# Summing the mean square per token, and moving the gate's modulation behind the fourth GLU pair

## The chip, the cores and the metric

The kernel runs on one core of a Trainium2 chip. The metric is device time in microseconds. The kernel before took 1121.05 us, the median of three runs (1117.35, 1121.05, 1123.47). The engines are named as the profile names them: PE is TensorE (PEld its weight loads), DVE is VectorE, ACT is ScalarE, POOL is GpSimd, SP is the engine that issues the DMAs here.

## What is computed

Two transformer blocks run one after the other on 512 tokens of width 1024. Only the entry of the first one matters here. `x` is normalised by its root mean square over the channels, scaled and shifted by a modulation that comes from the vector `c`, and projected; a third part of the modulation, `gate`, multiplies the block's output at its very end.

```
mod = silu(c) @ w_mod + b_mod
shift, scale, gate = split(mod, 3)
y = x * rsqrt(mean(x*x, axis=-1) + 1e-6)
u = (y * norm_w) * (1 + scale) + shift
p = u @ w_in          # q, k, v, attention gate, GLU halves, conv gate
a, g = split(p[GLU]); conv input = a * sigmoid(g)   # four pairs of 128 channels
...
h = x + gate * (concat(attention, conv) @ w_out)
```

## The kernel before

The kernel keeps channels on the partitions and tokens along the free axis: `x` is eight tiles `xs[j]` of 128 channels by 512 tokens. Each float32 product is made of three matmuls on rounded parts: a weight is split into `wh` (a rounded copy, made by ACT) and `wl` (the rest, made by DVE), the activations into the two tiles of `u`, and `mm3` multiplies high by high, high by low and low by high. Raw weights come in through two buffers (`wr`), the split ones stand in three (`wh`) and two (`wl`).

The instructions are written with a framework that orders them itself: a planner walks the program with its own estimate of every duration and, on each engine, takes the instruction that is ready and stands earliest in the program. So program order is a priority and not the order of execution, and each engine, the DMA issuer SP among them, then runs its list strictly in order. Only the depthwise convolution (`conv`) is marked to come later than its place in the program: its 120 multiply-adds on DVE fill what is free. Buffers of one tag are handed out in turn, and the next user of a buffer waits until the last reader of the one before is through. The PSUM tags of the first block are `pj` (one bank), `pv` (one), `pt` (two) and `s` (two pairs of banks).

The first block starts like this. Twelve matmuls on zeros (`warm_up`) open the PE. The eight tiles of `x` are loaded, then the modulation weights and the first raw weights. ACT squares each `xs[j]`, and PE multiplies the squares by a 128 x 128 matrix of 1/1024 (`ones`), adding the eight products in one `pj` bank: every partition then holds the mean square of all 512 tokens. ACT takes the root into `bs`, DVE the reciprocal of all 128 x 512 values.

The modulation is computed in six groups of 512 columns of `w_mod`. `mod_group` multiplies the vectors (32 columns, two used) with four loaded tiles, eight matmuls spread over the four 32-row strips of a `pj` bank; ACT copies the bank to `part`; four matmuls with two columns each turn the copy into per-partition scalars in a `pv` bank. `mod_pair` uses this for shift and scale of two channel tiles (groups 0 to 3), `mod_gate` for the gate (groups 4 and 5). Group 0 is done in two halves.

The loop `for j in range(KT)` then takes one channel tile after the other: it makes the modulation pair for every second j, `apply_mod` multiplies `xs[j]` by `bs` on DVE, scales and shifts it on ACT into `U` and takes the low part on DVE, and 18 matmuls add the products with six column blocks of the weights (`w_start`, three GLU pairs) into six banks `accs`: four on `s` and two on `pt`. After the loop, `glu` reads the three pairs (ACT a tanh, DVE a product), both gate groups are made, `conv` of the first three pairs is issued, and the fourth GLU pair is projected into `pj` and `pv` with the weights `w_in[0]` and `w_in[1]`, 24 matmuls each. The query projection (`q_ps`, on the banks `s`), the keys and values (on `pt`) and the attention with its gates (`zgate`, on `pj`, `pv` and `pt`) follow.

The helpers that the change newly calls exist before: `rsqrt` (ACT root, DVE reciprocal) and `bcast`, which spreads one column of per-token values over a row by a PE transpose for each 128 tokens. The context's norm (`norm_bs`) uses both with two columns.

Of the kernel before, what the change touches and what calls it, by code (L numbers as in the profile page):

```python
# [16 lines left out]
AF = mybir.ActivationFunctionType  # L17
# [5 lines left out]
P = 128  # L23
S = 512
D = 1024
KT = 8
# [198 lines left out]
def rsqrt(k, r, x, eps):  # L225
    k.A.activation(r, x, AF.Sqrt, bias=k.eps[eps])
    k.V.reciprocal(out=r, in_=r)
# [36 lines left out]
def bcast(k, r, n, tag):  # L264
    b = k.t(tag)
    for j in range(n):
        k.T.transpose(b[:, j * P:(j + 1) * P], r[:, j:j + 1].to_broadcast([P, P]), k.ident)
    return b
# [35 lines left out]
def setup1(k, I):  # L304
    k.rows = k.cal([6, 64])
    k.Y.dma_start(out=k.rows, in_=I["rows"].partition_broadcast(P))
    k.ones512 = k.cal([P])
    k.G.memset(k.ones512, 1.0 / 512)
    k.cw = small(k, k.vec("conv_w", 0, 124), 124, 0.5)
    k.hlw = small(k, k.vec("conv_ln_w", 0, 4), 4, 0.5)  # L310
    k.hlb = small(k, k.vec("conv_ln_b", 0, 4), 4, 0.5)
    k.bpw2 = small(k, k.vec("b_pw", 0, 4), 4, 2.0)
# [27 lines left out]
def block1(k, I, st, h1d):  # L340
    A, V, T, G, Y = k.A, k.V, k.T, k.G, k.Y
# [35 lines left out]
        Y.dma_start(out=t, in_=I["w_mod"][g, i])  # L377
        return t

    def mod_group(ts, e0=0, e1=2):  # L380
        ps = k.t("pj")
        o = slice(e0 * 256, e1 * 256)
        for kt in range(KT):
            q = 32 * (kt % 4)
            T.matmul(ps[q:q + 32, o], cc[:, kt, :], ts[kt // 2][:, kt % 2, o], start=kt < 4, stop=kt >= 4)
        part = k.t("tA")
        A.activation(part[:, o], ps[:, o], AF.Copy)
        cols = k.t("pv", [4, 2])
        for i in range(2 * e0, 2 * e1):
            T.matmul(cols[:, i, :], part[:, i * P:(i + 1) * P], k.sel32[:, 0:2], start=True, stop=True)  # L390
        return cols

    def mod_pair(g, ts, e0=0, e1=2):
        cols = mod_group(ts, e0, e1)
        for e in range(e0, e1):
            j = 2 * g + e
            V.tensor_scalar(out=shift[:, :, j], in0=cols[:, 2 * e, :], scalar1=k.vec("b_mod", j), scalar2=None, op0=ALU.add)
            V.tensor_scalar(out=A1[:, :, j], in0=cols[:, 2 * e + 1, :], scalar1=bm1[:, j:j + 1],
                            scalar2=k.vec("norm_w", j), op0=ALU.add, op1=ALU.mult)

    def mod_gate(g, ts):
        cols = mod_group(ts)
        V.tensor_tensor(out=gate[:, 4 * g - 16:4 * g - 12], in0=cols[:, :, 0], in1=k.vec("b_mod", 4 * g, 4), op=ALU.add)

    def norm_bs(vals, w, tag):
# [18 lines left out]
        V.tensor_tensor(out=lo, in0=t, in1=hi.bitcast(F32), op=ALU.subtract)  # L424
        return hi, lo

    ones = k.cal([P])
    G.memset(ones, 1.0 / D)
    ps = k.t("pj")
    for j in range(KT):  # L430
        sq = k.t("tA")
        A.activation(sq, xs[j], AF.Square)
        T.matmul(ps, ones, sq, start=j == 0, stop=j == KT - 1)
    bs = k.t("bs")
    A.activation(bs, ps, AF.Sqrt, bias=k.eps[1e-6])
    V.reciprocal(out=bs, in_=bs)
    a0, a1 = k.t("s", [2, S]), k.t("s", [2, S])
    accs = [a0[:, 0, :], a0[:, 1, :], a1[:, 0, :], a1[:, 1, :], k.t("pt"), k.t("pt")]
    us = []
# [1 line left out]
    mods = [[k.t("modw", [2, S]) for i in range(4)]]  # L441
# [36 lines left out]
    def glu(pa, pg):  # L478
        t = k.t("tA")
        A.activation(t, pg, AF.Tanh, scale=0.5)  # L480
        u2 = k.t("hg")
        V.scalar_tensor_tensor(out=u2, in0=t, scalar=1.0, in1=pa, op0=ALU.add, op1=ALU.mult)
        up.append(u2)
# [3 lines left out]
    def conv(i):  # L487
        u, cw = up[i], lambda w: k.cw[:, i * 31 + w:i * 31 + w + 1]
        y = ys[i] = k.t("hg")
        A.activation(y, u, AF.Identity, scale=cw(15), bias=k.vec("conv_b", i))  # L490
        with k.tc.high_priority(offset=-LATER):
            for w in range(31):
                if w != 15:
                    o0, o1 = max(0, 15 - w), min(S, S + 15 - w)
                    V.scalar_tensor_tensor(out=y[:, o0:o1], in0=u[:, o0 + w - 15:o1 + w - 15], scalar=cw(w), in1=y[:, o0:o1],
                                           op0=ALU.mult, op1=ALU.add)
# [4 lines left out]
    W1.fill(1)  # L501
    for i in range(3):
        glu(accs[2 * i], accs[2 * i + 1])
    for g in (4, 5):
        mod_gate(g, mods[g])
    setup1(k, I)
    k.rest()
    for i in range(3):
# [3 lines left out]
    proj(k, pg, W1.next(), us)  # L512
    glu(pa, pg)
    conv(3)

    q_ps = [k.t("s", [2, S]), k.t("s", [2, S])]
    for g in range(4):
        wh, wl = W1.next()
        for kk in range(2):
            j = 2 * g + kk  # L520
            c = slice(kk * S, (kk + 1) * S)
            for t in range(4):
                tt = slice(t * P, (t + 1) * P)
                uh, ul = us[j]
                ps = q_ps[t // 2][:, t % 2, :]
# [18 lines left out]
    for t in (2, 3, 4, 5, 0, 1):  # L544
        ps = k.t("pt", [256])
# [104 lines left out]
    for g in range(2):  # L650
        for o, ts_ in ((0, range(2, 6)), (512, range(0, 2))):
            b = k.t("pt")
# [120 lines left out]
    for pr in range(4):  # L773
        for half in range(2):
# [8 lines left out]
            if pend is not None:  # L783
                if pend[1] == 0:
                    pv = k.t("pv")
# [38 lines left out]
    for m in range(KT):  # L824
        if m % 2 == 0:
            wh, wl = W1.next()
        ps = oacc[m]
# [654 lines left out]
def emit(tc, I, out, dbg=None, stages=("b1", "b2", "ff")):  # L1482
    k = K(tc, dbg)
    nc = tc.nc
    with ExitStack() as st:
        k.open(st, "g", dict(g=1, wr=2, wh=3, wl=2))
        setup(k, I)
        h1d = nc.dram_tensor("h1d", (KT, P, S), F32, kind="Internal").ap()
        k.open(st, "H", dict(xa=6, xb=4, hg=16))
        p1 = ExitStack()  # L1490
        k.open(p1, "p1", dict(c1=1, U=16, tA=4, kvs=6))
        k.open(p1, "p1m", dict(pj=1), PSUM)
        k.open(p1, "p1s", dict(s=2), PSUM)
        k.open(p1, "p1t", dict(pt=2), PSUM)
        k.open(p1, "p1v", dict(pv=1), PSUM)
        if "b1" not in stages:
            k.rest()
        if "b1" in stages:
            nm = block1(k, I, p1, h1d)
        else:  # L1500
            nm = Norm(k, "norm_mix_g", "hg", "xb")
            for j in range(KT):
                x = k.x()
                k.Y.dma_start(out=x, in_=I["xT"][:, j, :])
                k.Y.dma_start(out=h1d[j], in_=x)
                nm.add(j, x)
        p1.close()
        k.nx = 0
        if "b2" in stages:
            k.open(st, "p2a", dict(c2=1, p=6, rk=4, v=2, z=2, bon=3, s8=6, nr=8))  # L1510
            k.open(st, "p2m", dict(pj=2), PSUM)
            k.consts("c2", 1350)
            block2(k, I, nm, h1d, out)
# [95 lines left out]
```

## Time and profile before

| | |
|---|---|
| runs | 1123.47, 1121.05, 1117.35 us; median 1121.05 us |
| the profiled execution | 1122.11 us, span 1120.3 us, mean granted PE clock 0.986 |
| PE busy | 1077.6 us, 96% of the span |
| PEld busy | 831.9 us, 74% |
| DVE busy | 727.6 us, 65% |
| ACT busy | 538.0 us, 48% |
| POOL busy | 61.8 us, 6% |

All times of the trace are microseconds from the start of the span. A granted clock of 1.00 is the PE's level of 2.4 GHz, 0.50 the level of 1.2 GHz. In a timeline row the bracket at the end says how long the engine had idled before and what ended it. A float32 matmul leaves two records. Every instruction of the kernel's helpers bears line 57, so instructions are told apart by their tiles: `s<-U,wh` is a matmul into `s` that reads `U` and `wh`. The span outside of the first 250 us (rest of the attention, output projection, second block and feed-forward) is not touched by the change.

### The profile page before, as it was taken

How to read it: one execution, taken by the hardware profiler on the slowest of the kernel's cores; microseconds unless marked ns; L12 is line 12 of the kernel's file. 1: busy time of each engine (PE TensorE's matmuls, PEld its weight loads, DVE VectorE, ACT ScalarE, POOL GpSimd, SP SyncE). 2: the span in 40 equal slices, each digit the busy share in tenths (PEclk: the TensorE clock that was granted, in tenths of full speed). 3: DMA queues.
4: the chain of work that ended last, by engine and by line, in shares of the span. 5: the costliest groups of instructions: out<-in, count | busy, mean ns of one | idle time of the engine just before them, and what ended most of it. 6: DMA issues, size and time to landing. Idle time of an engine off the chain costs nothing.

```text
span 1120.3 us, 15945 instructions
## 1 busy us (share of the span) xinstructions
PE 1077.6 (96%) x6272; PEld 831.9 (74%) x6272; DVE 727.6 (65%) x1267; ACT 538.0 (48%) x987; POOL 61.8 (6%) x209
## 2 busy tenths in 40 slices
PE   8999989999999999999999879999999999999998
PEld 4668966666787677777777657768888888888887
DVE  3369999995776889797867877666444344344332
ACT  5444546765655556555455655555333133134110
POOL 0000000000010201122101121010000000000000
PEclk9999999999999999999999998999999999999999
DMA  9753221001362110110011212122323333333332
GB/s 330 286 178 105 64 81 45 1 23 35 94 199 90 57 39 20 39 37 28 32 39 52 67 48 76 40 74 85 104 94 94 94 96 101 103 95 94 94 122 85
DMA packets 32203, 96.46 MB, mean 86 GB/s; under 512 B 3456, under 2 KB 6272, under 8 KB 32128
## 3 DMA queue, kind: packets, MB, share of 16 engines
q1 hardware_dynamic: 32128, 95.45, 26.5%
q8 instruction: 49, 0.80, 0.3%
q14 instruction: 26, 0.21, 0.1%
HBM read 91.24 MB, written 4.19 MB: 85 GB/s over the span
## 4 chain that ended last, share of the span: by engine, by line
PE 82%; DVE 6%; ACT 4%; POOL 3%; DMA 3%; issue 2%; SPq 0%; ACTq 0%; DVEq 0%; POOLq 0%
PE pf L57 31%; PE pj L57 22%; PE s L57 9%; PE i L57 7%; PE pt L57 5%; PE pv L57 4%; PE y L57 3%; POOL nr L57 3%; DMA modw<-w_mod 1%; ACT p L57 1%; DVE wl L57 1%; DVE hg L57 1%; ACT wh L57 1%; DVE p L57 1%; DMA wr<-w_in 1%
## 5 line engine op out<-in xcount | busy, mean ns | idle before, releaser
L57 ACT ACTIVATE wh<-wr 128x1024 fp32r<-128x1024 f32 (+1 forms) x132 | 137.7, 1043 | 183.7 <-PE pf L57 73.9
L57 DVE TENSOR_TENSOR wl<-wr,wh 128x1024 fp32r<-128x1024 f32 (+1 forms) x132 | 158.7, 1203 | 21.9 <-PE pt L57 10.2
L57 PE MATMUL pf<-A,wh 128*128 128x512 f32 x512 | 157.8, 389 | 0.0
L57 PE MATMUL pj<-hg,wh 128*128 128x512 f32 x448 | 152.5, 412 | 1.4 <-DVE x L57 0.9
L57 ACT ACTIVATE f<-i 128x512 f16<-128x512 f32 (+1 forms) x132 | 71.9, 598 | 90.1 <-PE i L57 89.9
L57 PEld LDWEIGHTS pf<-A,wh 128*128 128x128 f32 x512 | 96.0, 188 | 19.7
L57 PE MATMUL pf<-A,wl 128*128 128x512 f32 x256 | 99.6, 389 | 0.0
L57 DVE TENSOR_TENSOR x<-x,pf 128x512 f32<-128x512 f32 (+1 forms) x33 | 22.2, 671 | 113.9 <-PE pf L57 113.9
L57 PEld LDWEIGHTS pj<-hg,wh 128*128 128x128 f32 x448 | 80.2, 190 | 18.5 <-issue 2.2
L57 PE MATMUL pj<-hg,wl 128*128 128x512 f32 x224 | 90.2, 403 | 0.0
L57 DVE SCALAR_TENSOR_TENSOR hg<-hg,c 128x499 f32<-128x499 f32 (+14 forms) x120 | 84.9, 738 | 0.7 <-ACT hg L57 0.4
L57 PE MATMUL pf<-ff,wh 128*128 128x512 f32 (+1 forms) x272 | 79.6, 377 | 0.0
L57 PE MATMUL pf<-hg,wh 128*128 128x512 f32 x256 | 78.8, 389 | 0.0
L57 DVE SCALAR_TENSOR_TENSOR fr<-pf,r 128x512 f32<-128x512 f32 x32 | 22.1, 691 | 85.4 <-PE pf L57 82.1
L57 ACT ACTIVATE fr<-fr 128x512 f32<-128x512 f32 x32 | 20.2, 632 | 99.9 <-DVE fr L57 99.9
L57 PEld LDWEIGHTS <-f 128*128 128x128 f16 x720 | 46.8, 101 | 24.1 <-issue 13.7
L57 PE MATMUL i<-f 128*128 128x128 f16 x672 | 56.2, 226 | 5.3 <-DVE f L57 4.9
L57 PEld LDWEIGHTS pf<-ff,wh 128*128 128x128 f32 x272 | 50.1, 188 | 9.4
L57 PEld LDWEIGHTS pf<-A,wl 128*128 128x128 f32 x256 | 48.0, 188 | 10.1
L57 PEld LDWEIGHTS pf<-hg,wh 128*128 128x128 f32 x256 | 48.0, 188 | 9.9
L57 PE MATMUL pf<-ff,wl 128*128 128x512 f32 (+1 forms) x136 | 51.2, 376 | 0.0
L57 PE MATMUL pf<-hg,wl 128*128 128x512 f32 x128 | 49.8, 389 | 0.0
(312 smaller groups left out, 2114.8 us busy)
## 6 DMA issues: line engine op xcount, KB each, us to landing
wr<-w_ff SPq DMA_DIRECT2D x64, 512.0 KB, 3.5
modw<-w_mod SPq DMA_DIRECT2D x20, 512.0 KB, 7.6
wr<-rw_in SPq DMA_DIRECT2D x20, 512.0 KB, 3.6
wr<-w_in SPq DMA_DIRECT2D x10, 512.0 KB, 3.7
wr<-w_out SPq DMA_DIRECT2D x8, 512.0 KB, 3.6
wr<-w_start SPq DMA_DIRECT2D x8, 384.0 KB, 5.9
x<-xT SPq DMA_DIRECT2D x8, 256.0 KB, 5.8
modw<-w_mod SPq DMA_DIRECT2D x8, 256.0 KB, 6.2
```

The lines of the kernel that those rows point to most:

```text
L57: r = f(*a, **kw)
```

## The change

The squares become the stationary operand: for each of the eight squared tiles and each of the four 128-token blocks, one matmul with a single moving column of 1/1024 (`inv1k`) adds into one column of a `pt` bank (columns 0, 2, 4, 6), 32 matmuls in all. The tokens then lie on the partitions. `rsqrt` works on 128 x 4 values, `bcast` spreads the result with four transposes into the second `pt` bank, and ACT copies it to `bs`. The matrix `ones` and its memset are gone. The two gate groups move from behind the third GLU pair to behind the fourth one's `conv(3)`, ahead of the query projection, and take both of their banks from `pt` instead of `pj` and `pv`.

```diff
-    def mod_group(ts, e0=0, e1=2):
-        ps = k.t("pj")
+    def mod_group(ts, e0=0, e1=2, tags=("pj", "pv")):
+        ps = k.t(tags[0])
...
-        cols = k.t("pv", [4, 2])
+        cols = k.t(tags[1], [4, 2])
...
     def mod_gate(g, ts):
-        cols = mod_group(ts)
+        cols = mod_group(ts, tags=("pt", "pt"))
...
-    ones = k.cal([P])
-    G.memset(ones, 1.0 / D)
-    ps = k.t("pj")
+    ps = k.t("pt")
     for j in range(KT):
         sq = k.t("tA")
         A.activation(sq, xs[j], AF.Square)
-        T.matmul(ps, ones, sq, start=j == 0, stop=j == KT - 1)
+        for t in range(4):
+            T.matmul(ps[:, 2 * t:2 * t + 1], sq[:, t * P:(t + 1) * P], k.inv1k, start=j == 0 and t == 0, stop=j == KT - 1 and t == 3)
+    r = k.cal([4])
+    rsqrt(k, r, ps[:, 0:8:2], 1e-6)
+    b = bcast(k, r, 4, "pt")
     bs = k.t("bs")
-    A.activation(bs, ps, AF.Sqrt, bias=k.eps[1e-6])
-    V.reciprocal(out=bs, in_=bs)
+    A.activation(bs, b, AF.Copy)
...
     for i in range(3):
         glu(accs[2 * i], accs[2 * i + 1])
-    for g in (4, 5):
-        mod_gate(g, mods[g])
     setup1(k, I)
...
     glu(pa, pg)
     conv(3)
+    for g in (4, 5):
+        mod_gate(g, mods[g])
```

## Rows read from the trace of the kernel before

**Rows 1.** Page, busy time of each engine (us, share of span, instructions).
```profile
PE 1077.6 (96%) x6272; PEld 831.9 (74%) x6272; DVE 727.6 (65%) x1267; ACT 538.0 (48%) x987; POOL 61.8 (6%) x209
```
**Rows 2.** Chain of waits of the first 110 us: start, duration, what.
```profile
12.29 6.21 DMA modw<-w_mod
...
19.27 0.38 ACT tA L57
...
20.41 0.73 PE s L57 x2
...
74.98 5.59 PE pj L57 x24
```
**Rows 3.** Timeline, 6 to 23 us: start, duration, engine, instruction.
```profile
6.54 7.47 PE L57 MATMUL pj<-tA,c 128*128 128x512 f32 x16
...
14.10 0.69 ACT L57 ACTIVATE bs<-pj,g 128x512 f32<-128x512 f32 x1 [1.90 <-PE pj L57]
14.82 3.35 DVE L57 RECIPROCAL bs<-bs 128x512 f32<-128x512 f32 x1 [11.18 <-ACT bs L57]
...
22.07 0.14 PEld L57 LDWEIGHTS pj<-modw,c 128*32 128x32 f32 x4 [0.40 <-DMA modw<-w_mod]
```
**Rows 4.** Timeline, the context's norm at 104 us, with two columns.
```profile
104.28 0.26 ACT L57 ACTIVATE c<-pj,g 128x2 f32<-128x2 f32 x1
104.94 0.16 DVE L57 RECIPROCAL c<-c 128x2 f32<-128x2 f32 x1
...
105.62 0.38 PE L57 MATMUL pv<-g,c 128*128 128x128 f32 x2
```
**Rows 5.** PE timeline from 52 to 75 us.
```profile
52.66 1.92 PE L57 MATMUL pj<-modw,c 128*32 128x512 f32 x16
55.32 1.05 PE L57 MATMUL pv<-g,tA 128*128 128x2 f32 x8 [0.74 <-ACT tA L57]
56.30 1.92 PE L57 MATMUL pj<-modw,c 128*32 128x512 f32 x16
58.64 0.74 PE L57 MATMUL s<-U,wh 128*128 128x512 f32 x2 [0.41 <-ACT U L57]
...
60.21 0.50 PE L57 MATMUL s<-U,wh 128*128 128x512 f32 x1 [0.36 <-DVE U L57]
...
67.38 0.39 PE L57 MATMUL pt<-U,wl 128*128 128x512 f32 x1
69.01 1.05 PE L57 MATMUL pv<-g,tA 128*128 128x2 f32 x8 [1.25 <-ACT tA L57]
70.00 2.92 PE L57 MATMUL pj<-modw,c 128*32 128x512 f32 x16
...
74.84 0.71 PE L57 MATMUL pj<-U,wh 128*128 128x512 f32 x2
```
**Rows 6.** Windows: stretch, its length, busy by engine, PE clock, DMA.
```profile
16.00:20.00 4.00, 2.66 (x23) 1.26 (x23) 3.87 (x5) 1.38 (x4) 0.00 (x0) 1.00 1.06 391
...
70.00:71.00 1.00, 1.00 (x12) 0.32 (x15) 0.52 (x2) 1.00 (x2) 0.00 (x0) 0.89 0.84 137
70.00:75.00 5.00, 5.00 (x28) 2.33 (x28) 1.71 (x6) 2.60 (x4) 0.00 (x0) 0.66 0.37 107
80.00:150.00 70.00, 70.00 (x381) 60.90 (x380) 69.49 (x146) 34.01 (x62) 0.00 (x0) 1.00 0.27 85
...
156.00:160.00 4.00, 4.00 (x15) 3.05 (x13) 4.00 (x8) 3.71 (x13) 0.00 (x0) 0.57 0.30 115
```
**Rows 7.** ACT timeline at 61 us and DVE timeline at 75 us.
```profile
60.90 1.04 ACT L57 ACTIVATE wh<-wr 128x1024 fp32r<-128x1024 f32 x1
...
75.01 0.16 DVE L57 TENSOR_TENSOR c<-pv,g 128x4 f32<-128x4 f32 x1 [2.83 <-PE pv L57]
```
**Rows 8.** PE timeline around 155 and 165 us.
```profile
155.17 0.73 PE L57 MATMUL pj<-U,wh 128*128 128x512 f32 x2 [2.60 <-DVE hg L57]
...
165.88 0.73 PE L57 MATMUL s<-kst,xa 128*128 128x512 f32 x2 [0.83 <-ACT xa L57]
```

## The prediction

> **What bounds the kernel now.** I read the page's busy times first, then the chain of waits of the first 110 us, the timelines of the stretches that the change touches, and the granted clock by windows. PE is busy for 96% of the span [rows 1]. So a microsecond taken out of a PE wait early on reaches the end, unless a later wait swallows it. Three stretches count.
>
> (a) The start, up to the first product with `w_start` at 20.41. The chain runs through the loads of the modulation weights, until 18.50, the PE and ACT work on the second half of modulation group 0 (ACT copy at 19.27), `U`, and that matmul [rows 2]. The reciprocal, 14.82 to 18.17 [rows 3], is not in the chain.
>
> (b) 52 to 75 us. At j = 6 the PE waits for the modulation's ACT and DVE steps between 54.58 and 58.64. In that hole lie eight two-column records (55.32 to 56.37) and, at 56.30, sixteen records of the first gate group, which fill 1.92 us of it. At 67.61 (the last loop matmul starts at 67.38, and one starts every 0.23) the PE stops until 69.01, does the rest of the gate work and two query matmuls, and reaches the fourth pair at 74.84: 7.23 us between the loop and the pair [rows 5].
>
> (c) 75 to 160 us. DVE is busy 69.49 of 70 us while PE is full too [rows 6]. At 155.17 the PE has waited 2.60 us for a DVE product [rows 8], and after that hole the clock is 0.57 for 4 us [rows 6].
>
> **The change, part by part.** The sums are made against the profiled execution's 1122.11 us (span 1120.3), which is 1.06 above the median of the runs.
>
> *Mean square.* Before, eight matmuls of two records each take 6.54 to 14.01, then a root of 0.69 and a reciprocal of 3.35 [rows 3]: `bs` is ready at 18.17. After, there are 32 matmuls of one column, 64 records. The nearest row has two columns: eight records from 69.01 to the next start at 70.00, so 0.124 each [rows 5], 7.9 us together. They start at 6.5, behind the warm-up, and end at about 14.4; the last square ends 1.90 before ACT's root, at 12.20 [rows 3], so the squares don't hold them up. Then root 0.26, reciprocal 0.16, four transposes 0.62 (two take 0.38 [rows 4], I add 0.12 for each more), a copy like `bs`'s of 0.6, four handoffs of 0.05: 16.3, or 17.3 where the first half of group 0 goes ahead of the transposes (16 records of half the columns of those that take 1.92 [rows 5]). `bs` is 0.9 to 1.9 us earlier. What is late next is what was late before: the weights that land at 18.50, and the pair-1 weights for which the PE waits again at 22.07 [rows 3]. If the planner keeps ACT's order (copy of the second half ahead of `U`), the gain is nothing. If `U` goes first, the 2.24 between `bs` and the PE's start lose that copy (0.38) and a wait of some 0.3 for it; 17.3 + 1.6 is 18.9, and 1.5 is gained. I take 0.5, nearer to the order that the trace has.
>
> *The clock at the start.* The ones-matmuls kept the PE streaming 512 columns from 6.5 to 14; 64 one-column records do not. The one place where the trace shows such work, a wait of 1.25 and eight two-column records, is followed by a clock of 0.89 in 70 to 71 and 0.66 over 70 to 75, which is (1 - 0.66) x 5 = 1.7 us of full speed [rows 5, 6]. So I expect a low clock from about 10 us on. It makes the weight work of group 0 slower, but that waits for loads anyhow, and the records of `w_mod` alone kept a clock of 1.00 in 16 to 20 us with 2.66 of 4 us busy [rows 6], so it can lift the clock again. Cost 0 if it has risen by 20 us, 1.7 if the loop's first matmuls run low. I take 0.5. The start comes out even: 0, from -1.5 to +1.7.
>
> *The hole at j = 6.* The first gate group can no longer lie there: its banks are now `pt`, and both hold `accs` until the third GLU pair is read, after 67.4. The fourth pair cannot take its place either, since its first weights are split only from 60.90 us on [rows 7]. The wait itself stays as long (U is not earlier). But 4.06 us with nothing except eight two-column records is more than what preceded the fall at 70 [rows 5]. The low clock would meet the matmuls from 58.64 and 60.21 on. Bounds: 0 (no fall) and 1.7 (a low stretch like that of 70 to 75 wholly on dense work). I take +1.3, because some of it is spent inside the hole.
>
> Here the Trainium skill, "TensorE: Matmul & The Clock Gate", section "Why this matters for your kernels", speaks of idle gaps longer than any single one here as those that send the clock down. By it the +1.3 would be 0. The fall at 70, behind a gap of only 1.25 us with two-column work around it, says otherwise, and I go by that.
>
> *The gate groups.* Off the path go the wait from 67.61 to 69.01 (1.4) and the low clock (1.7). On the path comes the first group's weight part, which was hidden: 16 records, 1.8 by pitch. Everything else is only moved into the query projection, with copies by ACT (idle there: 34 of 70 us busy [rows 6]) covered by query matmuls. 1.4 + 1.7 - 1.8 gives -1.3. If the planner puts the two-column parts straight behind the copies, the PE waits twice for about 1.25 as at 69.01, and the term is +1.2; if the moved work finds holes, it is -3.1. The DMAs are not moved: the gate's weights are issued in the loop as before, and only the context's later tiles take their buffers. The loads on SP and the small products on POOL that `setup1` issues now stand ahead of the gate groups and read nothing of them.
>
> *DVE.* The gate's small addition at 75.01 made DVE wait 2.83 us for the PE, with convolution steps queued behind it [rows 7]. Moved behind the fourth pair, it comes when DVE has a full queue, so I expect DVE to be about 2.8 earlier against the loop's end, the PE 1.3. The hole before 155.17 shrinks by 2.83 - 1.3 = 1.5, from 2.60 to about 1.1, and then it should not bring the clock down: (1 - 0.57) x 4 = 1.7 more [rows 6]. Only about half of that counts, since the start of the attention at 165.88 hangs on DVE and ACT steps [rows 8] and not on PE alone. I take -1.5 - 0.9 = -2.4. Bounds: 0, if the moved additions make DVE wait as long elsewhere, and -4.3 (2.60 + 1.7).
>
> Sum: 0 + 1.3 - 1.3 - 2.4 = -2.4. On the profiled execution that is 1119.7; on the median 1118.6.
>
> **Rivals.**
> 1. *The clock eats it* (slower). Place: the one-column sums and the emptied hole at j = 6. Price: 1.7 at each, and DVE finds new waits on the gate's additions, so that its term is 0: 1.7 + 1.7 - 1.3 = +2.1, 1123.2; with two low stretches in a row at the start 1.7 more, 1124.9. It decides from the point where the clock is still low at 23 us, when the loop's matmuls run without a break. For it: the fall at 70. Against it: 1.00 in 16 to 20 us on a half-busy PE [rows 6].
> 2. *The clock holds and everything is gained* (faster). No low stretch, `U` goes first, the hole at 155 and the low clock after it vanish: -1.5 - 1.3 - 4.3 = -7.1, 1114.0. For it: the reciprocal and DVE's wait are real idle time of others. Against it: the loads at 18.50 and 22.07 stay. (By the rule that the Trainium skill gives in the section named above, the part of this rival at j = 6 would hold.)
> 3. *Only the order changes.* The reciprocal was hidden by the loads and the gate's work by nothing new, so the change does not do what it says; but the planner places every later instruction by its own times, and these shift. What such an order is worth is bounded by the hole of 2.60 and the low stretch of 1.7 behind it, one of each more or less: 1114 to 1123, and with a second such pair in a later part as far again on either side.
>
> **How the numbers follow.** A difference of 0.5%, 5.6 us, is about what a measurement of this kernel can tell from no change: faster means below 1115.4, slower above 1126.7. Forecast (1116.5 to 1121): 0.45. Rival 1: 0.2, of which 0.06 past 1126.7 when the runs' own spread (6.1 us over three) is added. Rival 2: 0.22, of which 0.16 below 1115.4. Rival 3: 0.13, 0.05 below, 0.06 above. The forecast's own tail gives 0.03 below. Faster 0.24, same 0.64, slower 0.12. The range runs from a little below rival 2, 1112, to a little above rival 1, 1126.
>
> **What would show it.** `bs` written by an ACT copy at 16 to 18 us, and the first matmul with `U` between 18.9 and 20.5. A granted clock below 1.00 somewhere in 10 to 20 us and again about 57 to 62. The fourth pair's first matmul within 0.3 us of the loop's last one. No DVE wait of 2.8 us at 75. The gate's weight records among query matmuls with no PE wait over 0.5. A PE hole of at most 1.5 us near 150 and no low clock behind it. The forecast is wrong if the clock stays low into the loop, if DVE waits for the gate's columns, or if the hole near 150 is as long as before.

## The result and the profile after

The changed kernel takes 1137.9 us (median of 4 runs, 1134.57 to 1140.84) beside 1121.57 for the kernel before: a ratio of 1.0147, 95% interval 1.0121 to 1.0174. It is 16 us slower. The forecast was 1118.6, the range 1112 to 1126, and slower had a chance of 0.12. The profiled execution took 1140.84 us, with a span of 1138.8 and a mean granted clock of 0.974.

The page's line of busy times, which answers to [rows 1]:

```profile
PE 1094.0 (96%) x6324; PEld 846.5 (74%) x6324; DVE 725.1 (64%) x1267; ACT 539.1 (47%) x988; POOL 61.7 (5%) x208
```

PE is busy 16.4 us longer, and its share has stayed. So it waits only some 2 us more in sum (span less busy time, 44.8 against 42.7); for the rest it works more slowly or at other work. The chain of waits shows where that begins (start, duration, what; it answers to [rows 2]):

```profile
7.72 11.82 PE pt L57 x56
19.54 0.99 PE pj L57 x2
20.52 1.05 PE pt L57 x4
21.57 1.89 PE pj L57 x14
...
23.55 0.39 ACT tA L57
...
25.48 0.82 ACT U L57
```

Before, this stretch hung on a DMA until 18.50. Now the sums themselves are the chain: 56 records in 11.82 us, 0.211 each, and nearly all of the first half of modulation group 0 comes behind them. The granted clock by windows (columns as in [rows 6]: stretch, length, busy by engine in the order PE, PEld, DVE, ACT, POOL, clock, DMA):

```profile
8.00:14.00 6.00, 6.00 (x30) 6.00 (x31) 0.00 (x0) 3.33 (x6) 0.00 (x0) 0.50 1.04 362
14.00:20.00 6.00, 6.00 (x28) 5.62 (x28) 0.13 (x1) 0.26 (x1) 0.00 (x0) 0.50 1.06 383
20.00:28.00 8.00, 7.09 (x32) 3.59 (x30) 2.80 (x7) 4.07 (x6) 0.00 (x0) 0.50 0.45 161
28.00:45.00 17.00, 15.22 (x81) 8.21 (x80) 5.30 (x12) 4.07 (x6) 0.00 (x0) 0.98 0.78 282
45.00:49.00 4.00, 3.86 (x7) 1.40 (x8) 2.29 (x4) 3.88 (x6) 0.00 (x0) 0.58 0.27 110
72.00:76.00 4.00, 3.62 (x10) 2.55 (x10) 1.39 (x3) 3.33 (x4) 0.00 (x0) 0.61 1.01 367
...
171.00:176.00 5.00, 4.62 (x15) 3.66 (x16) 5.00 (x12) 3.62 (x12) 0.00 (x0) 0.66 0.34 105
```

From 8 to 28 us the clock is 0.50, the level of 1.2 GHz, while PE and PEld are busy nearly all the time up to 20. In the first 182 us three more falls follow, two in the loop and one behind the convolution. The timeline of the same kernel, with the rows that answer to [rows 3, 5, 7 and 8] (start, duration, engine, instruction; in brackets the idle time before it and what ended that):

```profile
5.59 1.05 PE L57 MATMUL pt<-g,tA 128*128 128x1 f32 x8
7.72 11.82 PE L57 MATMUL pt<-g,tA 128*128 128x1 f32 x56 [1.07 <-ACT tA L57]
...
19.87 0.18 DVE L57 RECIPROCAL c<-c 128x4 f32<-128x4 f32 x1 [16.25 <-ACT c L57]
...
26.34 1.22 PE L57 MATMUL s<-U,wh 128*128 128x512 f32 x2 [0.35 <-ACT U L57]
...
32.38 0.63 PE L57 MATMUL pj<-modw,c 128*32 128x256 f32 x4
...
35.44 0.73 PE L57 MATMUL s<-U,wh 128*128 128x512 f32 x2 [0.35 <-ACT U L57]
...
40.95 1.06 PE L57 MATMUL pj<-modw,c 128*32 128x512 f32 x6
...
45.14 0.84 PE L57 MATMUL s<-U,wh 128*128 128x512 f32 x2 [0.35 <-ACT U L57]
...
56.27 1.06 PE L57 MATMUL pj<-modw,c 128*32 128x512 f32 x6
...
60.90 0.73 PE L57 MATMUL s<-U,wh 128*128 128x512 f32 x2
...
71.73 0.73 PE L57 MATMUL s<-U,wh 128*128 128x512 f32 x2 [1.35 <-ACT U L57]
...
81.86 0.39 PE L57 MATMUL pt<-U,wl 128*128 128x512 f32 x1
...
94.59 1.92 PE L57 MATMUL pt<-modw,c 128*32 128x512 f32 x14
...
98.47 0.16 DVE L57 TENSOR_TENSOR c<-pt,g 128x4 f32<-128x4 f32 x1 [1.50 <-PE pt L57]
...
171.38 0.80 PE L57 MATMUL pj<-U,wh 128*128 128x512 f32 x2 [3.75 <-DVE hg L57]
...
182.07 0.73 PE L57 MATMUL s<-kst,xa 128*128 128x512 f32 x2 [0.83 <-ACT xa L57]
```

Three things are to be read here. The reciprocal has become cheap (0.18 in place of 3.35), but it starts at 19.87, later than the old one ended. The first product of the loop comes at 26.34 (before 20.41). And in the loop the PE now leaves its products four times for modulation work and the ACT and DVE steps behind it (32.38 to 35.44, 40.95 to 45.14, 56.27 to 60.90, 70.3 to 71.73); before it did so twice (30.54 to 35.18, 52.66 to 58.64). Such a stretch, in which the products wait for the steps of a modulation group, is called an open hand-off here. The first of the two in the kernel before:

```profile
30.54 1.07 PE L57 MATMUL pj<-modw,c 128*32 128x512 f32 x8
...
35.18 0.72 PE L57 MATMUL s<-U,wh 128*128 128x512 f32 x2
```

In the traces the loop lasts 55.9 us (26.34 to 82.25) instead of 47.4 (20.41 to 67.77). The attention's first product (`s<-kst`) is 16.2 us late (182.07 against [rows 8]'s 165.88), and from there to the second block's first matmul both kernels need nearly the same, 186.8 and 186.4. So nearly all of the 18.5 us between the two traces is lost in the first 182 us: about 5.9 up to the loop's first product, 8.5 in the loop, 1.7 behind it.

### The profile page after: what moved, and what is told of

Same layout as the page of the kernel before. It is cut to its first block, busy times and chain, and to the rows that moved or that the text cites. A ratio compares the mean times of both kernels' runs of the same rounds, so it can differ in the third digit from the quotient of the medians.

```text
span 1138.8 us, 16036 instructions
## 1 busy us (share of the span) xinstructions
PE 1094.0 (96%) x6324; PEld 846.5 (74%) x6324; DVE 725.1 (64%) x1267; ACT 539.1 (47%) x988; POOL 61.7 (5%) x208
## 4 chain that ended last, share of the span: by engine, by line
PE 82%; DVE 7%; ACT 4%; POOL 3%; issue 2%; DMA 2%; SPq 0%; ACTq 0%; DVEq 0%; POOLq 0%
PE pf L57 31%; PE pj L57 21%; PE s L57 9%; PE i L57 8%; PE pt L57 7%; PE pv L57 4%; PE y L57 3%; POOL nr L57 3%; DVE wl L57 1%; DVE hg L57 1%; ACT p L57 1%; DMA wr<-w_in 1%; DVE p L57 1%; ACT xb L57 1%; DVE c L57 1%
## 5 line engine op out<-in xcount | busy, mean ns | idle before, releaser
L57 PEld LDWEIGHTS pj<-hg,wh 128*128 128x128 f32 x448 | 80.4, 190 | 18.4 <-issue 2.2
L57 DVE SCALAR_TENSOR_TENSOR hg<-hg,c 128x498 f32<-128x498 f32 (+14 forms) x120 | 84.7, 736 | 0.3
```

Source lines behind the costliest of these rows:

```text
L57: r = f(*a, **kw)
```

## The experiments

Three theories were on record. CLOCK: the one-column sums send the PE's clock down, and that costs. PLAN: the planner, walking the program with other durations, puts the modulation groups of the loop in other places, and these cost. GATES: the gate groups cost at their new place. Each result lists the span and mean granted clock of every run, so time can be split: span x (1 - clock) is what is lost to the low clock (idle time at the low level included), span x clock is the rest. The table has the means over the runs of a kernel; beside these kernels the kernel before had 13.6 to 16.1 lost and a rest of 1104.2 to 1105.4. From run to run of one kernel the lost part differs with a standard deviation of 1.5 to 4.4 us, the rest with one of 0.5 to 1.9.

| kernel | median us | ratio to before, 95% interval | lost to the clock | rest |
|---|---|---|---|---|
| changed | 1137.9 | 1.0147 [1.0121, 1.0174] | 26.1 | 1109.6 |
| e1 new sums, old gates | 1132.28 | 1.0113 [1.0085, 1.0141] | 21.5 | 1109.1 |
| e2 old sums, moved gates | 1128.06 | 1.0067 [1.0041, 1.0094] | 18.7 | 1107.0 |
| e3 128 columns, moved gates | 1124.41 | 1.0036 [1.0011, 1.0061] | 15.7 | 1107.4 |
| e4 changed, half 1 early | 1133.3 | 1.0107 [1.0083, 1.0131] | 25.7 | 1105.0 |
| e5 before, groups late | 1129.81 | 1.0068 [1.0041, 1.0094] | 16.4 | 1111.6 |
| e6 128 columns, old gates | 1123.93 | 1.0023 [0.9999, 1.0047] | 15.2 | 1106.4 |
| e7 e3 with groups late | 1127.65 | 1.0047 [1.0024, 1.0071] | 15.2 | 1111.1 |
| e8 e3, one gate group moved | 1121.65 | 0.9998 [0.9979, 1.0016] | 11.7 | 1108.0 |
| e9 changed, zero matmuls between | 1135.04 | 1.0123 [1.0094, 1.0151] | 19.6 | 1114.5 |
| e10 old sums, one gate group moved | 1127.01 | 1.0047 [1.0025, 1.0068] | 18.4 | 1107.1 |
| e12 128 columns, groups placed by hand | 1120.18 | 0.9973 [0.9958, 0.9988] | 13.0 | 1105.1 |
| e13 e12 with one column | 1130.76 | 1.0075 [1.0054, 1.0096] | 26.2 | 1102.7 |
| e14 changed, longer opening | 1138.22 | 1.0141 [1.0106, 1.0175] | 25.8 | 1109.6 |
| e15 e1, longer opening | 1134.33 | 1.0109 [1.0064, 1.0153] | 23.8 | 1108.6 |

By this split some 10 to 12 of the 16 us are clock, and some 4 to 5 are not.

**The two halves alone.** e1 has only the new sums, e2 only the moved gates (both as in the diff above).

> The new sums alone; the gate groups stay where they were, on their old banks. Three theories of the lost 16 us. CLOCK: the one-column matmuls let the granted clock fall from 8 to 29 us, the sums end 5.5 us later, and what follows at the start runs slow. PLAN: the planner, given other durations at the start, places the modulation groups of the loop so that four hand-offs stand open instead of two, and the loop lasts 8.5 us longer. GATES: the moved gate groups lie on the path between the fourth pair and the queries (94.6 to 102.2 us). CLOCK and PLAN together expect 1134 to 1139 here, nearly all of the loss; GATES expects 1122 to 1126.

> The old sums; the gate groups alone are moved behind the fourth pair, on the pt banks. GATES expects 1129 or more. CLOCK and PLAN expect no loss here: 1118 to 1124, the gate work on the path (+7.6) against the 7.2 us between loop and fourth pair that go. The prediction's own terms for this half are +1.3 (clock at j = 6), -1.3 and -2.4, so 1119.2.

Both are slower, and their losses, 11.0 and 6.8 us, add up to a little more than the whole, 16.3. Neither came out as one theory alone had it: e1 stayed below the 1134 of CLOCK and PLAN, e2 above the 1124 that these two gave it and just below the 1129 of GATES. In e1's timeline the records take 10.99 us, 0.172 for each of the 64, since the clock falls only at 10.3, and the groups lie in the loop as in the changed kernel:

```profile
6.51 10.99 PE L57 MATMUL pt<-g,tA 128*128 128x1 f32 x64
...
25.22 1.08 PE L57 MATMUL pj<-modw,c 128*32 128x256 f32 x8
...
30.18 0.63 PE L57 MATMUL pj<-modw,c 128*32 128x256 f32 x4
...
33.25 0.73 PE L57 MATMUL s<-U,wh 128*128 128x512 f32 x2 [0.35 <-ACT U L57]
```

In e2 they lie as before (30.46 and 52.60). So the new order of the loop is a consequence of the sums, not of the gates. e2's timeline shows what the gates do:

```profile
58.58 0.73 PE L57 MATMUL s<-U,wh 128*128 128x512 f32 x2 [2.26 <-ACT U L57]
...
68.80 0.62 PE L57 MATMUL pj<-U,wh 128*128 128x512 f32 x2
...
87.43 0.16 DVE L57 TENSOR_TENSOR c<-pt,g 128x4 f32<-128x4 f32 x1 [1.00 <-PE pt L57]
...
156.19 1.22 PE L57 MATMUL pj<-U,wh 128*128 128x512 f32 x2 [3.33 <-DVE hg L57]
...
233.47 1.65 PE L57 MATMUL s<-kst,xa 128*128 128x512 f32 x4 [1.84 <-ACT p L57]
...
294.91 0.73 PE L57 MATMUL pj<-U,wh 128*128 128x512 f32 x2 [1.90 <-ACT wh L57]
```

```profile
60.00:64.00 4.00, 3.85 (x11) 3.09 (x12) 0.79 (x2) 3.13 (x4) 0.00 (x0) 0.65 0.92 326
155.00:162.00 7.00, 5.81 (x16) 4.56 (x17) 5.93 (x14) 4.10 (x14) 0.00 (x0) 0.51 0.23 75
```

The hole at j = 6 is empty and is followed by a low clock (second fence, e2's windows). The fourth pair starts 0.22 after the start of the loop's last matmul. The hole behind the convolution is longer than before, not shorter, with 7 us of low clock. And the attention, which no edit touches, has got another order of its matmuls. In it stands a wait of 1.84 with a low stretch behind it (0.83 from 230 to 240), and one of 1.90 for a split weight, where the longest of that kind in the kernel before is 0.94. A wait like the first the kernel before has too, but its clock stayed at 1.00 from 230 to 240:

```profile
230.42 0.98 PE L57 MATMUL s<-kst,xa 128*128 128x512 f32 x4 [1.74 <-ACT p L57]
```

**The width of the moving operand.** e3, e6: the same 32 matmuls, but each moves all 128 columns of the old matrix, and the root reads one column of each 128.

```diff
-T.matmul(ps[:, 2 * t:2 * t + 1], sq[:, t * P:(t + 1) * P], k.inv1k, ...)
+T.matmul(ps[:, t * P:(t + 1) * P], sq[:, t * P:(t + 1) * P], ones, ...)
-rsqrt(k, r, ps[:, 0:8:2], 1e-6)
+rsqrt(k, r, ps[:, 0:S:P], 1e-6)
```

> The changed kernel, but each of the 32 summing matmuls moves 128 equal columns of 1/1024 instead of one, and the root reads one column of each 128. The same work is done behind it. CLOCK expects the clock to stay at 1.00 over 6 to 20 us, the sums to end at 14 to 15 us (19.5 in the changed kernel), and the time to fall by 5 to 7 us: 1131 to 1133 if the loop stays as long as it is. The planner's order of the loop changes here as well (half of group 0 goes ahead of the loop's products); PLAN expects a further 4 to 8 us of gain, 1123 to 1128. GATES expects 1136 or more.

> The new sums with 128 moving columns, the gate groups where they were before the change. If the two halves of the change add up (sums alone +11, gates alone +6.8), this is the wide kernel of the last run less the gates' share: 1116 to 1119, faster than before. If the gates' loss comes only together with the old sums, 1122 to 1125.

128 times the columns cost next to nothing and save 13.5 us of the changed kernel's 16: the sums end at 14.3 in both traces, where one column ended at 19.5. e6's window shows the clock at the same kind of work. In the 8 to 14 us of it PE and PEld are busy for 6.00 of 6 us, as in the changed kernel, but the clock is 1.00 and not 0.50:

```profile
6.00:14.00 8.00, 7.15 (x64) 6.96 (x63) 0.00 (x0) 5.39 (x9) 0.00 (x0) 1.00 1.02 330
```

But the width also changes what the planner sees, and so the places of the groups in the loop. e4, e5 and e7 take the places apart.

**The places of the groups.** e4 issues the second half of group 0 ahead of the first product. e5 is the kernel before with the last weight matmuls of the second half and of groups 1 and 2 tied behind the products of the tile (`k.after`), and the column matmuls of group 3 too. e7 does the same in e3.

```diff
 # e4
-        if j < 2:
-            mod_pair(0, mods[0], j, j + 1)
+        if j == 0:
+            mod_pair(0, mods[0], 0, 1)
+            mod_pair(0, mods[0], 1, 2)
 # e5, e7, in mod_group
-            T.matmul(ps[q:q + 32, o], ...)
+            r = T.matmul(ps[q:q + 32, o], ...)
+            if kt >= late:
+                k.after(r, k.mm)
```

> The changed kernel with its one-column sums; only the second half of modulation group 0 stands ahead of the first tile's modulation in the program, so that the planner takes it before the loop's products, as in the kernel before. The clock at the start stays low. PLAN expects one or two of the four open hand-offs to go: 3 to 6 us, 1131 to 1135. CLOCK alone expects no more than 1 us: 1136 to 1138.

> The kernel before with its old sums and old gates; only the last weight matmuls of the second half of group 0 and of groups 1 and 2, and the two-column matmuls of group 3, are tied behind the loop products that precede them in the changed kernel, so that the modulation groups stand on the PE as the planner put them there. No one-column matmuls, the clock at the start stays as it was. PLAN expects the loop to last 6 to 8 us longer: 1127 to 1130. CLOCK expects 1120 to 1123.

> The whole change with 128 moving columns, so that the clock is held, and with the modulation groups tied into the places that they have in the changed kernel. It differs from the changed kernel by the width of the moving operand alone, and from the wide kernel (1124.4) by the places of the groups alone. PLAN expects 1129 to 1133 (open hand-offs cost 5 to 8 us with any clock). CLOCK expects 1124 to 1127 (the hand-offs cost little; 11 to 13 of the 16 us were the clock).

e4 has the same sums and the same low clock as the changed kernel (25.7 lost) and a rest of 1105.0, that of the kernel before. So the places make 4.6 of the 16 us. e7 has the places of the changed kernel's loop and only the width different: 1127.65 and 1137.9, 10.3 for the width. In e7's attention 4.9 us are lost that the changed kernel does not lose (below); up to the attention's first product the two traces differ by 10.6 (171.49 and 182.07). For the same reason the 3.2 between e7 and e3 is not all the loop's: e7's attention starts 1.7 later in the traces. e5 gives 8.3, but it is no exact copy: with the old sums early, the product queue meets waits for `U` that the changed kernel has not, such as 1.83 before the first product. CLOCK and PLAN both hold, CLOCK with the larger share: 10.3 to 10.6 for the width, 4.6 for the places.

**The gates, taken apart.** e8 (on e3) and e10 (on e2) leave group 4 where it was and move only group 5.

```diff
-    for g in (4, 5):
-        mod_gate(g, mods[g])
+    mod_gate(4, mods[4])      # behind the third GLU pair, on pj and pv
...
+    mod_gate(5, mods[5], ("pt", "pt"))   # behind conv(3)
```

> The new sums with 128 moving columns; the first gate group stays in its old place on its old banks, where its weight matmuls can fill a hole of the loop, only the second goes behind the fourth pair on the pt banks. If the gates' loss is the emptied hole and the clock after it, this takes back some 3 of the 6.8 us: 1118 to 1122. If it is the place behind the fourth pair that costs, it stays at 1123 to 1125.

> The old sums; the first gate group in its old place on its old banks, only the second behind the fourth pair on the pt banks. It differs from the kernel with the gates alone moved (1128.1) by the first group. If that loss is the hole at j = 6, emptied, and the low clock behind it with what follows from both, 1120 to 1124. If it is the place behind the fourth pair, 1126 to 1129.

e8 is even with the kernel before. e10 keeps the hole at j = 6 filled (its loop ends at 66.84) and still takes 1.0047. Its timeline has the same two waits in the attention as e2's:

```profile
230.23 1.65 PE L57 MATMUL s<-kst,xa 128*128 128x512 f32 x4 [1.84 <-ACT p L57]
...
291.71 0.73 PE L57 MATMUL pj<-U,wh 128*128 128x512 f32 x2 [1.89 <-ACT wh L57]
```

Between the attention's first product and the second block e2 needs 190.2 us, e10 190.6 and e7, which has these two waits as well, 191.7; before, changed, e1, e3, e8 and e12 need 186.4 to 187.7. The sequence of matmuls in the attention is the same in e2, e7 and e10, and another one in the kernel before, changed, e1, e3 and e6 (e8 and e12 have a third). So about 3.8 of the 6.8 us of e2 are another order of the attention, which the planner takes in some of the kernels with moved gates and not in others. GATES as a fixed price of 6.8 for the new place falls: in the whole times the gates cost 6.8 on the old sums, 5.6 or 3.9 on one-column sums (changed against e1, e14 against e15) and 0.5 on wide ones (e3 against e6), which can't be told from nothing. A smaller price is not excluded. From the loop's first product to the second block the kernel with moved gates needs longer in the traces of every pair: 2.1 us for e2 without the 3.8, 2.8 for changed against e1, 1.5 for e14 against e15, 2.6 for e3 against e6. What the 3.9 to 5.6 of the whole times consist of is not shown; by the table more than half of it is clock.

**Holding the clock from outside.** e9 adds three zero matmuls of 512 columns behind the four of each tile in the changed kernel.

```diff
+        for _ in range(3):
+            T.matmul(hold, warm[:, 0:P], warm, start=True, stop=True)
```

> The changed kernel with one moving column as it is, and behind each tile's four summing matmuls three matmuls of 512 columns on zeros (24 in all, 0.21 each at the high level: 5.1 us of added work whose result nobody reads). The modulation groups keep their places. CLOCK expects the granted clock to stay at 1.00 behind the warm-up, the one-column records to come back from 0.21 to about 0.13 each, so that the sums with 5.1 us of added work end no later than they do now (19 to 20 us), and the time at 1132 to 1137, not above the changed kernel's 1137.9. If one-column matmuls are slow at any clock, the added work comes on top: 1141 to 1145.

e9's timeline shows the pace of the one-column records at either level, as the clock falls in its middle:

```profile
15.28 0.95 PE L57 MATMUL pt<-g,tA 128*128 128x1 f32 x8
16.09 0.74 PE L57 MATMUL pj<-bs 128*128 128x512 bf16 x2
16.62 1.71 PE L57 MATMUL pt<-g,tA 128*128 128x1 f32 x8
```

```profile
15.00:16.00 1.00, 1.00 (x10) 0.90 (x9) 0.00 (x0) 0.00 (x0) 0.00 (x0) 1.00 1.11 356
16.00:17.00 1.00, 1.00 (x8) 0.80 (x7) 0.00 (x0) 0.00 (x0) 0.00 (x0) 0.70 1.08 361
17.00:18.00 1.00, 1.00 (x7) 1.00 (x7) 0.00 (x0) 0.00 (x0) 0.00 (x0) 0.50 1.08 407
```

Eight records last 0.95 at 1.00 and 1.71 with the clock at 0.50 but for their start. From the start of the first to the start of what follows it is 0.81 at 1.00, 0.101 each; the changed kernel's 56 records at 0.50 come to 0.21 each. The zero matmuls held the clock until 16.4 (CLOCK had it held throughout; it is low from there to about 30) and took 6.5 us off what is lost, but put 4.9 us of work in (rest 1114.5), so that little is gained.

**One gap at the start.** In the changed kernel the PE idled 1.07 us behind its first eight records, in e1 it did not, and e1's clock fell later. e14 and e15 have four more opening matmuls.

```diff
-WARM = 12
+WARM = 16
```

> The changed kernel with 16 zero matmuls at the start instead of 12, the places of all other instructions unchanged. START (in the changed kernel the opening matmuls ended at 5.75, eight one-column records ran, and the PE idled 1.07 us before the rest; the clock fell at 8.1. In the kernel with the sums alone there was no such idle time and it fell only at 10.3 and rose again at 20.5 for 3.4 us): with the gap covered, the records run on without a break, the clock falls at about 10, the sums end near 17.5 to 18, the first loop product comes at 24 to 25.5 instead of 26.3, and the time is about 1134 to 1135. Rival, RECORDS (the one-column records alone set the length of the low stretch, and it lasts into the first loop products wherever it begins): sums end at 19 to 19.5, the first product at 26 or later, and the time stays at 1137 to 1139.

> The one-column sums alone with the gate groups at their old place, and 16 zero matmuls at the start instead of 12. START: this kernel had no gap at its start in its profiled run, so it stays at 1131 to 1133. The difference to the changed kernel with 16 zero matmuls is then the price of the moved gate groups on top of one-column sums: 2 to 3 us by START, because about 3 of the 5.6 seen so far belonged to the gap at the start; 5 to 6 by GATES (the gate groups themselves cost that much at their new place).

START is not borne out by the medians. e14 stays at 1138.22, what the rival gave. Its one trace, of the fastest of its four runs (1134.98), does look as START expected, with 0.31 of the gap left: the clock falls at about 12.3, the sums end at 16.59 and the first product comes at 23.40. But two of the changed kernel's four runs were as fast without the longer opening (1134.57, 1135.2). e15 has no gap, and its clock is low from about 9.9 to about 30.4 in its trace, longer than e1's; its 1134.33 lies above START's 1131 to 1133. When the clock falls and when it rises again differs between traces of the same sums (their end lies between 16.59 and 19.67 in six of them), and the gap alone does not decide it. What does is open.

**A version by hand.** e12 has wide sums, both halves of group 0 at j = 0, groups 1 to 3 ahead of the products of j = 1, 3 and 5, gate group 4 ahead of those of j = 7, and group 5 behind the fourth pair. So every group's ACT and DVE steps lie beside products that are ready. e13 is e12 with one column.

```diff
+        if j % 2 == 1 and j < 6:
+            mod_pair(j // 2 + 1, mods[j // 2 + 1])
+        if j == 7:
+            mod_gate(4, mods[4])
```

> An attempt at a faster version, from what PLAN says. Sums with 128 moving columns; each modulation pair, and the first gate group, stands one step ahead in the program: half 2 of group 0 before the first tile, pairs 1, 2 and 3 before the products of tiles 1, 3 and 5, the first gate group before those of tile 7; the second gate group behind the fourth pair on the pt banks. PLAN expects the loop from 19.2 us to last 32.8 (144 products of 0.23) + some 11 for the groups: its end at 63 to 65 (67.8 before), the queries 6 to 8 us earlier, and 1112 to 1117 in all. If DVE, which is full from 80 to 150 us, sets that stretch, half of it is lost: 1116 to 1120. If the hand-offs cost nothing, 1121.

> As the run before it, with one moving column instead of 128 and nothing else changed; the modulation groups have the same places. The difference of the two is the width alone, on a loop without open hand-offs. CLOCK expects +6 to +11 over that run (sums that end 4 to 5 us later, and the first products at the low level). If the clock's part of the loss was only the planner's places, 0 to +2.

e12 is the fastest of all, 0.9973 of the kernel before, with an interval that ends below 1; but that is 2.3 us, less than the 3 that are read as an effect here (see the end of the next section). It missed its forecast of 1112 to 1117: its loop ends at 66.56 instead of 63 to 65, its attention starts 2.8 us earlier than before (163.12) and then lasts 1.2 longer. Its timeline and windows show sums that end at 14.3 and a clock of 1.00 through the sums and the loop:

```profile
7.85 6.52 PE L57 MATMUL pt<-c,tA 128*128 128x128 f32 x56 [0.69 <-ACT tA L57]
14.30 1.05 PE L57 MATMUL pj<-modw,c 128*32 128x256 f32 x10
```

```profile
6.00:14.00 8.00, 7.31 (x65) 7.09 (x64) 0.00 (x0) 5.35 (x9) 0.00 (x0) 1.00 1.03 360
...
20.00:40.00 20.00, 19.71 (x100) 12.64 (x100) 9.76 (x18) 9.52 (x13) 0.00 (x0) 1.00 0.87 338
40.00:67.00 27.00, 26.73 (x144) 19.41 (x143) 10.64 (x22) 13.37 (x18) 0.00 (x0) 1.00 0.72 264
```

A record of 128 columns takes 0.115 us from start to start (7.85 to 14.30 for 56). From 20 to 67 us the PE idles 0.6 us, where the kernel before idled 2.4 from 20 to 66. Between e12 and e13 only the width differs: 10.6 us, made of 13.2 more lost to the clock and 2.4 less of the rest.

## Why the prediction was wrong, step by step

*Mean square: failed in a size.* The step was: 64 records by 0.124, 7.9 us, end at 14.4. The price came from a row at the full level. There it is more than enough (0.101 in e9), and the wide sums did end at 14.3; but 56 of the 64 one-column records ran at 0.50 and took 0.211 each, so they ended at 19.54. The rest of the step's chain stood: reciprocal 0.18, transposes 1.05 at the low clock (0.65 in e12), copy 0.60.

*The clock at the start: the step that failed.* The prediction saw the low clock coming, and from about 10 us; the rows show about 8. It then costed it as something that falls on other work behind the sums, capped at 1.7, and left the sums' own pitch at the full level. The fall lay on the very records that caused it. Where the places are kept alike, the low clock is worth 10.6 us (e13 against e12). The argument that `w_mod` records with a half-busy PE kept 1.00 in 16 to 20 us [rows 6], "so it can lift the clock again", did not carry: from 20 to 28 us such records ran at 0.50 in the changed kernel, and the clock rose only when the loop's products were running. In the traces of e1 and e13 it did rise among such records, at about 20.5, and fell again at 24.

The Trainium skill, "TensorE: Matmul & The Clock Gate", Part 1 (The HAM clock gate), says that the clock is set by how busy the PE has been. Here, from 8 to 14 us, the profile has PE and PEld busy for 6.00 of 6 us at 0.50 in the changed kernel and for 6.00 of 6 at 1.00 in e6: the busy time of the profile is not that measure.

*The hole at j = 6: right.* +1.3 was taken; e2's loop takes 48.65 us, 1.3 more than before, and the clock is 0.65 in 60 to 64. The rule of the Trainium skill, "TensorE: Matmul & The Clock Gate", section "Why this matters for your kernels", which warns of longer idle gaps only, did not hold here: 2.26 us of idle time, with two-column records ahead of it, were followed by the fall. The length of a wait does not settle it either: behind e2's wait of 1.90 (294.91) the clock stayed at 1.00, behind the like wait of 1.91 in e7 (298.56) it was 0.66 from 298 to 303. In the changed kernel this term does not stand by itself, because the loop has another order.

*The gate groups: right.* -1.3 was taken. From the end of the loop to the key projection e2 needs 39.13 us, the kernel before 40.15: -1.0. The pair follows the loop at once, and the two-column records cost no PE wait.

*DVE: wrong in sign.* -2.4 was taken; from the key projection to the attention e2 needs 59.8 us and the kernel before 58.0, so +1.8. The step that failed is that DVE would be 2.8 earlier against the loop's end: the PE's first product behind the hole comes 87.2 us after the loop's end in e2, 87.4 before, so DVE gained 0.2. As the PE was 1.0 earlier, the hole grew, to 3.33 in e2 (3.75 in the changed kernel) instead of 2.60, and the low stretch behind it with it. The additions wait for the PE at their new place too (1.00 at 87.43 in e2, 1.50 at 98.47 in the changed kernel); both of e2's together cost DVE 1.6 us, against 3.1 before, and other waits took up the rest, such as one of 1.05 for ACT at 135.00 that the kernel before does not have. With the terms as measured, +1.3 - 1.0 + 1.8, the moved gates cost 2.1 in e2's trace, where the prediction's terms give -2.4.

*The order of the loop: not in the sum.* The text followed the planner's choice only at one point, whether `U` goes ahead of a copy. The later sums let it open two more hand-offs. In the profiled execution the loop lasts 8.5 us longer. Two low stretches within it (0.58 in 45 to 49, 0.61 in 72 to 76) are (1 - 0.58) x 4 + (1 - 0.61) x 4 = 3.2 of them, the low clock from 26.3 to 28.5 another 1.1, and the hand-offs, which sum to 13.2 us and before to 10.6, another 2.6; 1.6 is not accounted for. Rival 3 named this mechanism and bounded it by one hole and one low stretch, 4.3 us, and twice that with a second pair; e4 puts the places at 4.6. What rival 3 lacked was the clock at the start.

Rival 1 had the right sign and both places, at an eighth to a quarter of the price, 2.1 to 3.8 us. Its deciding point was met: the clock was low at 23 us.

What is not settled: why the planner takes the slower order of the attention in e2, e7 and e10, and what decides when the clock falls and rises at the start. The low stretches of the second block also differ from run to run, which is why differences below 3 us between two of these kernels are not read as effects.

## What to carry to other kernels

A matmul of one moving column is hardly cheaper than one of 128 when each has its own 128 x 128 weight load: here a record took 0.101 us (e9) and 0.115 us (e12) at the full level, and only the wide one kept that level. When a change takes streaming columns off the PE, price its remaining records at the low level first, then ask whether anything keeps the clock up. And where a planner orders the work, a change of durations at the start can change the order of everything behind it: write down which hand-offs lie open before and after, and place the groups by hand if they matter.

## What the runs showed of the hardware that was not expected

- A stretch of one-column float32 matmuls with PE and PEld busy for 6.00 of 6 us ran at a granted clock of 0.50; the same stretch with 128 columns, as busy, ran at 1.00 (e6, 8 to 14 us).
- A record of weight load and one-column matmul takes 0.101 us from start to start at 1.00 (e9) and 0.21 at 0.50 (changed). The weight load follows the clock as well: one of 128 x 128 float32 lasts 0.19 us at 1.00 and 0.33 at 0.50 (e1).
- The clock fell behind waits of 2.26 us (e2, j = 6) and 3.33 us (e2, behind the convolution), both in the middle of dense work. A wait of 1.9 us was followed by a fall in e7 and by none in e2.
